# Attention scores in row pairs and values in float32: one edit of a diffusion block on one core

## The chip, the cores and the metric

The kernel runs on one core of one Trainium2 chip. The metric is the device time of one execution, in microseconds (us). A measurement is a set of runs; the median and the ends are given. Beside them stands one execution that the hardware profiler took; the rows in this document come from that one.

## What is computed

Two layers work on 512 latent tokens and 256 context tokens of width 1024. The edit lies in the first layer's token mixer, differential attention with 8 heads: each head has two maps of 64 dimensions, whose softmaxes are taken one from the other. Cut to what matters:

```python
def attend(qb, kk, vv):
    s = jnp.einsum('bqhmd,bkhmd->bhmqk', qb, kk).astype(jnp.float32) * scale
    p = jax.nn.softmax(s, axis=-1)
    p = p[:, :, 0] - lam_full * p[:, :, 1]
    return jnp.einsum('bhqk,bkhe->bqhe', p.astype(vv.dtype), vv)
```

Here m is the map (0 or 1), d runs over 64, k over 768 keys (512 latent, 256 context) and e over the 128 columns of a head's values. Only latent queries (512) matter. After it come an RMS norm of each head's output, the output projection, a SwiGLU FFN, and a second layer with a short convolution and another FFN.

## The kernel before, in words

Everything is float32. For speed the matmuls run on the one-pass type fp32r, and each operand is split in a high part (rounded to fp32r, on ScalarE, ACT) and a low part (the rest, on VectorE, DVE): `split`, L53 to L55. A product is then three matmuls, high x high, high x low and low x high: `mm3`, L77 to L80.

The stages in order of time: modulation weights, norms and transposes of the inputs with the projections of head 0 (to some 104 us of the profiled execution); the attention of 8 heads with the projections of later heads and the output projection between (to some 420 us); then FFN, convolution and FFN, which are long streams of matmuls.

One head of the attention (`attend`, L508) loops over two halves of the queries (`pr`), and in each over two blocks of 128 queries (`s`), so that there are 32 blocks in all. For a block and each of the two maps, four matmuls write the scores S (128 queries x 768 keys, in two ranges of columns, 512 and 256, in two PSUM banks); DVE takes the negative maximum of a row (L532); ACT takes the exponential and its sum (L536). DVE then adds the two maps with their weights (L546), six transposes on TensorE (PE) bring the result to keys x queries (L551), and `split` writes its two parts `pth` and `ptl` (L553). After two blocks the values are multiplied: 6 blocks of keys x `mm3` of 256 columns into `po` (L556 to L558), copied to O by ACT.

How S is computed before: a map has only 64 dimensions, so the 128 rows of a matmul hold two things. `finish_q` (L442) and `finish_k` (L451) apply the rotary positions (`rope`, with POOL, that is GpSimd, and DVE), split the result into `qt` and `kt`, and `halves_to` (L432) copies the parts by eight DMAs for a head on SyncE's queue (SP): `qs0` and `qs1` hold a map's q twice, one above the other, high parts and low parts side by side; `ks0` and `ks1` hold the high part of k in the upper 64 rows and the low part in the lower. One matmul of 128 rows so gives q_high x (k_high + k_low), a second q_low x (k_high + k_low).

The values of two heads at a time are projected by `proj_v_steps` and split by `finish_v` (L461) into `vh` and `vl`, six tiles each. Head 0 and the first values come from PSUM of the first stage.

PSUM has eight banks: two buffers of two banks for S, two for the accumulators of projections ("acc"), two for transposes, `po` and small things ("pt").

What sets the order: nothing is written out by hand. The generators in `todo` (projections of the next heads, modulation vectors `ada_steps`, the output projection `wo_steps`) are stepped through after each head in the program's text, and a scheduler in the framework, which works with modelled times, mixes all instructions into one fixed order for each engine ahead of the run. Each engine then works its list in that order. All loads and copies are issued from SP's queue, in order too.

Of the kernel before, what the change touches and what calls it, by code (L numbers as in the profile page):

```python
# [11 lines left out]
F32 = mybir.dt.float32  # L12
F32R = mybir.dt.float32r
# [5 lines left out]
P = 128  # L19
# [5 lines left out]
def block_kernel(  # L25
# [11 lines left out]
    nc = tc.nc  # L37
    T = x.shape[1]
# [4 lines left out]
    KV = T + C  # L43
    KB = KV // P
# [8 lines left out]
    def split(hi, lo, src):  # L53
        nc.scalar.copy(hi, src)  # L54
        nc.vector.tensor_tensor(lo, src, hi.bitcast(F32), op=ALU.subtract)  # L55
# [21 lines left out]
    def mm3(ps, sh, sl, mh, ml, start, stop):  # L77
        nc.tensor.matmul(ps, sh, mh, start=start, stop=False)  # L78
        nc.tensor.matmul(ps, sh, ml, start=False, stop=False)  # L79
        nc.tensor.matmul(ps, sl, mh, start=False, stop=stop)  # L80
# [30 lines left out]
    psB = tc.alloc_tile_pool(name="psB", bufs=2, space=PSUM)  # L111
# [8 lines left out]

    for tag, n, bufs in (
        [(f"Or{h}", 512, 1) for h in range(NH)] + [("qs0", 1024, 2), ("qs1", 1024, 2)]
        + [("e", 768, 3), ("pth", 768, 3), ("ptl", 768, 3), ("ks0", 768, 2), ("ks1", 768, 2)]
        + [(f"v{p}{t}", 256, 2) for t in range(KB) for p in "hl"]
        + [("sq", 512, 1), ("dg0", 512, 1), ("dg1", 512, 1)]
        + [(t, 4, 2) for t in ("sv", "sr", "rh", "rl")] + [(t, 4, 3) for t in ("rr", "mx")] + [("ss", 8, 2), ("den", 8, 2)]
        + [("ld", 2, 1)]
        + [("araw", 1024, 2), ("ada", 1024, 1), ("qt", 1024, 1), ("kt", 1536, 1), ("rcos", 512, 1), ("rsin", 512, 1)]
        + [("sw", 512, 1), ("rt", 512, 2)]
    ):  # L130
        ap.tile([P, n], F32, tag=tag, bufs=bufs, name=f"place_{tag}")
# [4 lines left out]
    xt_dram = nc.dram_tensor("xt_spill", [DB, P, T], F32, kind="Internal").ap()  # L136

    rows = lambda v: v.rearrange("(j p) -> j p", p=P)
    st1, st2 = (ap.tile([P, P], F32, tag=t, name=n) for t, n in (("ks1", "st1"), ("ks1", "st2")))
    nc.vector.memset(st1, 0.0)  # L140
    nc.vector.memset(st2, 0.0)
    nc.sync.dma_start(st1[0:8, :], rows(c[0]))
# [26 lines left out]
    cn = [nat(ctx, t, "qs1", 2, f"cn{t}") for t in range(CB)]  # L169
# [37 lines left out]
    def nat_rstd(src, tag, name):  # L207

        nb = len(src)
        ss = ap.tile([P, 8], F32, tag="ss", name=f"ss{name}")  # L210
        for t in range(nb):
            for f in range(2):
                junk = ap.tile([P, 512], F32, tag="sq", bufs=1, name=f"junk{name}")
                nc.scalar.activation(
                    junk, src[t][:, f * 512:(f + 1) * 512], AF.Square,
                    accum_out=ss[:, t + 4 * f:t + 4 * f + 1],
                )
        v = ap.tile([P, 4], F32, tag="sv", name=f"sv{name}")[:, :nb]
        nc.vector.tensor_tensor(v, ss[:, :nb], ss[:, 4:4 + nb], op=ALU.add)
        nc.vector.tensor_scalar(v, v, 1.0 / D, EPS, op0=ALU.mult, op1=ALU.add)  # L220
        r = ap.tile([P, 4], F32, tag="sr", name=f"sr{name}")[:, :nb]
        nc.gpsimd.tensor_tensor(r, v, mhalf[:, :nb], op=ALU.pow)
        ps = spread(r, nb, "pt", name)
        o = ap.tile([P, 512], F32, tag=tag, bufs=2 if tag == "ks0" else 1, name=f"rs{name}")[:, :nb * P]
        nc.vector.tensor_copy(o, ps)
        return o

# [40 lines left out]
    for k in range(0, DB, 2):  # L268
        pt = psB.tile([P, 2, T], F32, tag="S", name=f"ptx{k}")
# [3 lines left out]
            nc.vector.tensor_copy(XT0[k + a], pt[:, a, :])  # L273
        if k == 0:
            ada0(0, raws0)
    rc = nat_rstd(cn, "ks0", "c")
    ctt = [ap.tile([P, 4, C], F32, tag="araw", name=f"ct{i}") for i in range(2)]
    CT = [ctt[k // 4][:, k % 4, :] for k in range(DB)]
    for i in range(2):
        pt = psB.tile([P, 4, C], F32, tag="S", name=f"ptc{i}")  # L280
        for a in range(4):
            k = 4 * i + a
# [146 lines left out]
        eng.tensor_tensor(r, r, s, op=ALU.add)  # L429
        return r  # L430

    def halves_to(dst, src, both):  # L432

        for m in range(2):
            s = src[64 * m:64 * m + 64]
            for d in range(2):
                o = dst[m][64 * d:64 * d + 64]
                nc.sync.dma_start(
                    o.bitcast(F32), (s if both else s[:, d, :]).bitcast(F32)
                )  # L440

    def finish_q(h, ps):  # L442

        r = rope(ps, HD ** -0.5, f"q{h}")
        qt = ap.tile([P, 2, T], F32R, tag="qt", bufs=1, name=f"qt{h}")
        split(qt[:, 0, :], qt[:, 1, :], r)
        q = [ap.tile([P, 2, T], F32R, tag=f"qs{m}", name=f"qs{h}_{m}") for m in range(2)]
        halves_to(q, qt, True)
        return q

    def finish_k(h, ps, psc):  # L451

        r = rope(ps, None, f"k{h}")
        kt = ap.tile([P, 2, KV], F32R, tag="kt", bufs=1, name=f"kt{h}")
        split(kt[:, 0, T:], kt[:, 1, T:], psc)
        split(kt[:, 0, :T], kt[:, 1, :T], r)
        ks = [ap.tile([P, KV], F32R, tag=f"ks{m}", name=f"ks{h}_{m}") for m in range(2)]
        halves_to(ks, kt, False)
        return ks

    def finish_v(g, t, ps):  # L461
        vh = ap.tile([P, 256], F32R, tag=f"vh{t}", name=f"vh{g}_{t}")
        vl = ap.tile([P, 256], F32R, tag=f"vl{t}", name=f"vl{g}_{t}")
        split(vh, vl, ps)
        return vh, vl

    def v_load(g):
        cols = slice(2 * D + 256 * g, 2 * D + 256 * (g + 1))
# [39 lines left out]
    def attend(h, between, after=None):  # L508
        q, ks, vs = Q[h], K[h], V[h // 2]
        vc = slice((h % 2) * P, (h % 2) * P + P)  # L510
        O = ap.tile([P, T], F32, tag=f"Or{h}", bufs=1, name=f"O{h}")
        den = ap.tile([P, 2, TB], F32, tag="den", name=f"den{h}")
        for pr in range(2):
            pts = []
            for kh in range(2):
                pts.append(
                    (ap.tile([P, 3, 256], F32R, tag="pth", bufs=3, name=f"pth{h}_{pr}_{kh}"),
                     ap.tile([P, 3, 256], F32R, tag="ptl", bufs=3, name=f"ptl{h}_{pr}_{kh}"))
                )
            for s in range(2):  # L520
                qb = 2 * pr + s
                e = []
                mx = ap.tile([P, 2], F32, tag="mx", bufs=3, name=f"mx{h}_{qb}")
                for m in range(2):
                    S = psB.tile([P, 1024], F32, tag="S", name=f"S{h}_{qb}_{m}")
                    for a, b in ((0, 512), (512, KV)):
                        for j in range(2):
                            nc.tensor.matmul(  # L528
                                S[:, a:b], q[m][:, j, qb * P:(qb + 1) * P], ks[m][:, a:b],
                                start=(j == 0), stop=(j == 1),  # L530
                            )
                    nc.vector.tensor_reduce(  # L532
                        out=mx[:, m:m + 1], in_=S[:, :KV], axis=AX.X, op=ALU.max, negate=True
                    )
                    em = ap.tile([P, KV], F32, tag="e", bufs=3, name=f"e{h}_{qb}_{m}")
                    nc.scalar.activation(  # L536
                        em, S[:, :KV], AF.Exp, bias=mx[:, m:m + 1], accum_out=den[:, m, qb:qb + 1]
                    )
                    e.append(em)

                rr = ap.tile([P, 1], F32, tag="rr", bufs=3, name=f"rr{h}_{qb}")
                nc.vector.reciprocal(rr, den[:, 1, qb:qb + 1])
                nc.vector.scalar_tensor_tensor(
                    rr, rr, nlam, den[:, 0, qb:qb + 1], op0=ALU.mult, op1=ALU.mult
                )
                nc.vector.scalar_tensor_tensor(e[0], e[1], rr, e[0], op0=ALU.mult, op1=ALU.add)  # L546
                for kh in range(2):
                    pt = psB.tile([P, 512], F32, tag="pt", name=f"pt{h}_{qb}_{kh}")[:, :3 * P]
                    for i in range(3):
                        k = 3 * kh + i  # L550
                        nc.tensor.transpose(pt[:, i * P:(i + 1) * P], e[0][:, k * P:(k + 1) * P], ident)  # L551
                    cs = slice(s * P, (s + 1) * P)
                    split(pts[kh][0][:, :, cs], pts[kh][1][:, :, cs], pt.rearrange("p (k c) -> p k c", c=P))  # L553
                between()
            po = psB.tile([P, 512], F32, tag="pt", name=f"po{h}_{pr}")[:, :256]
            for k in range(KB):  # L556
                ph, pl = pts[k // 3]
                mm3(po, vs[k][0][:, vc], vs[k][1][:, vc], ph[:, k % 3, :], pl[:, k % 3, :], k == 0, k == KB - 1)  # L558
            nc.scalar.copy(O[:, pr * 256:(pr + 1) * 256], po)
            if after:  # L560
                On[h] = O
                after(pr, den)
        On[h] = O
        if not after:
            later.append(subnorm(h, den, 0, TB))
# [395 lines left out]
```

## Time and profile before

| what | value |
|---|---|
| median of 3 runs | 1371.27 us (1370.04 to 1371.96) |
| the profiled execution | 1369.84 us |
| its span, first to last instruction | 1368.1 us |
| mean granted clock of PE in it | 0.987 of full |
| PE, DVE, ACT, POOL busy | 96%, 57%, 39%, 18% of the span |

The profile's page has a table of engines with their busy time, and the span in 40 slices with a digit for each engine (9 is 90% or more). A timeline row has the start, the time until the end, the engine, the line, the operation with what it writes and reads, the tile of the array (rows*columns), the shape, and how many instructions were merged. PEld is the load of a matmul's stationary operand, which runs beside PE. Matmuls are pipelined: the next starts before the one ahead has ended, so the step from start to start is what a matmul costs.

### The profile page before, as it was taken

Reading aid. Unit: us, or ns where it says so; the run is one execution under the profiler, and the core shown is the slowest. Engines: PE = TensorE matmul, PEld = TensorE weight load, DVE = VectorE, ACT = ScalarE, POOL = GpSimd, SP = SyncE. Lnnn points to the kernel's source line nnn. Section 1 sums busy time; section 2 is a strip of 40 time slices with the busy share of each in tenths; the row PEclk is TensorE's granted clock in tenths of the full one; section 3 lists DMA queues with packets and bytes.
Section 4 is the critical chain, followed back from the end, with each engine's and each line's share of the span. In section 5 each row is a group of like instructions: output and inputs, shape, how many; then the busy total and the mean of one; then the engine's idle time right before and its main releaser. Section 6 shows DMA issues by size and latency. Waiting matters only on the chain.

```text
span 1368.1 us, 18008 instructions
## 1 busy us (share of the span) xinstructions
PE 1312.1 (96%) x7052; PEld 1128.1 (82%) x7052; DVE 780.4 (57%) x1043; ACT 529.6 (39%) x872; POOL 244.8 (18%) x197
## 2 busy tenths in 40 slices
PE   6889899899999999999999999999999999999997
PEld 4678799798888988888888889888988888888887
DVE  6886976777886766776753255444473333332322
ACT  6655646454555432333222244222362232232222
POOL 3244635524314100000001041000340000000000
PEclk9999999999999999999999999999999999999999
DMA  8957633623432666666643333333333333333321
GB/s 291 271 151 219 189 101 124 152 80 93 135 97 80 197 206 200 219 222 203 212 128 96 100 93 93 93 98 88 92 93 99 102 92 93 106 91 109 94 78 62
DMA packets 238742, 182.79 MB, mean 134 GB/s; under 512 B 6937, under 2 KB 220226, under 8 KB 238658
## 3 DMA queue, kind: packets, MB, share of 16 engines
q1 hardware_dynamic: 238658, 181.65, 44.7%
q8 instruction: 55, 0.90, 0.3%
q14 instruction: 29, 0.24, 0.1%
HBM read 162.75 MB, written 4.19 MB: 122 GB/s over the span
## 4 chain that ended last, share of the span: by engine, by line
PE 79%; DVE 8%; DMA 4%; ACT 4%; issue 2%; POOL 2%; SPq 0%; DVEq 0%; ACTq 0%; POOLq 0%
PE po_fo L78 6%; PE po_fo L79 6%; PE po_fo L80 6%; PE pb L79 5%; PE pb L78 5%; PE pb L80 5%; PE pa L78 5%; PE pa L79 5%; PE pa L80 5%; DMA araw<-in_ada_w_dram 3%; PE S L528 2%; PE psc L79 1%; PE psb L80 1%; PE psu L80 1%; PE psc L80 1%
## 5 line engine op out<-in xcount | busy, mean ns | idle before, releaser
L54 ACT CAST whi_f<-raw_f 128x1024 fp32r<-128x1024 f32 x87 | 91.4, 1051 | 234.6 <-issue 117.9
L55 DVE TENSOR_TENSOR wlo_f<-raw_f,whi_f 128x1024 fp32r<-128x1024 f32 x87 | 107.4, 1234 | 79.2 <-ACT whi_f L54 76.2
L55 DVE TENSOR_TENSOR wlo_fo<-raw_fo,whi_fo 128x1024 fp32r<-128x1024 f32 (+1 forms) x48 | 54.5, 1135 | 118.4 <-ACT whi_fo L54 116.8
L607 POOL TENSOR_TENSOR nacc<-nacc,nsq 128x256 f32<-128x256 f32 x30 | 30.7, 1023 | 494.1 <-ACT nsq L603 493.6
L78 PE MATMUL po_fo<-uh,whi_fo 128*128 128x512 f32 (+1 forms) x324 | 118.8, 367 | 0.1
L79 PE MATMUL po_fo<-ul,whi_fo 128*128 128x512 f32 (+1 forms) x324 | 118.7, 366 | 0.0
L80 PE MATMUL po_fo<-uh,wlo_fo 128*128 128x512 f32 (+1 forms) x324 | 118.6, 366 | 0.0
L54 ACT CAST whi_fo<-raw_fo 128x1024 fp32r<-128x1024 f32 (+1 forms) x48 | 47.1, 981 | 177.6 <-PE po_fo L79 146.9
L378 DVE SCALAR_TENSOR_TENSOR ada<-araw,sil,ada 128x1024 f32<-128x1024 f32 x49 | 62.9, 1284 | 39.0 <-DMA araw<-in_ada_w_dram 38.7
L803 DVE TENSOR_TENSOR uu<-sl,pb 128x512 f32<-128x512 f32 (+1 forms) x48 | 30.7, 640 | 81.5 <-PE pb L80 77.2
L536 ACT ACTIVATE e<-S,mx 128x768 f32<-128x768 f32 x64 | 57.8, 904 | 46.7 <-DVE mx L532 36.1
L80 PE MATMUL pb<-h2h,wlo_f 128*128 128x512 f32 (+1 forms) x192 | 71.8, 374 | 0.0
L78 PE MATMUL pa<-h3h,whi_f 128*128 128x512 f32 (+1 forms) x192 | 71.6, 374 | 0.0
L79 PE MATMUL pb<-h2l,whi_f 128*128 128x512 f32 (+1 forms) x192 | 71.5, 372 | 0.0
L78 PE MATMUL pb<-h2h,whi_f 128*128 128x512 f32 (+1 forms) x192 | 71.4, 372 | 0.0
L78 PE MATMUL pb<-h3h,whi_f 128*128 128x512 f32 (+1 forms) x192 | 71.4, 372 | 0.0
L79 PE MATMUL pb<-h3l,whi_f 128*128 128x512 f32 (+1 forms) x192 | 71.4, 372 | 0.0
L80 PE MATMUL pa<-h3h,wlo_f 128*128 128x512 f32 (+1 forms) x192 | 71.4, 372 | 0.0
L80 PE MATMUL pb<-h3h,wlo_f 128*128 128x512 f32 (+1 forms) x192 | 71.4, 372 | 0.0
L79 PE MATMUL pa<-h3l,whi_f 128*128 128x512 f32 (+1 forms) x192 | 71.2, 372 | 0.0
L78 PEld LDWEIGHTS po_fo<-uh,whi_fo 128*128 128x128 f32 x324 | 61.2, 189 | 10.1 <-DVE on L890 0.3
L79 PEld LDWEIGHTS po_fo<-ul,whi_fo 128*128 128x128 f32 x324 | 61.1, 189 | 9.9
(362 smaller groups left out, 3715.2 us busy)
## 6 DMA issues: line engine op xcount, KB each, us to landing
raw_f<-in_ffn_w_in_dram SPq DMA_DIRECT2D x88, 512.0 KB, 3.6
araw<-in_ada_w_dram SPq DMA_DIRECT2D x80, 512.0 KB, 4.4
raw_fo<-in_ffn_w_out_dram SPq DMA_DIRECT2D x32, 512.0 KB, 3.7
raw_a<-in_ada_w_dram SPq DMA_DIRECT2D x32, 256.0 KB, 4.6
qs<-qt SPq DMA_DIRECT2D x32, 256.0 KB, 4.9
raw_wv<-in_da_wqkv_dram SPq DMA_DIRECT2D x12, 512.0 KB, 5.0
ks<-kt SPq DMA_DIRECT2D x32, 192.0 KB, 4.8
raw_fo<-in_ffn_w_out_dram SPq DMA_DIRECT2D x16, 384.0 KB, 4.0
```

The source lines that it names most:

```text
L54: nc.scalar.copy(hi, src)
L55: nc.vector.tensor_tensor(lo, src, hi.bitcast(F32), op=ALU.subtract)
L78: nc.tensor.matmul(ps, sh, mh, start=start, stop=False)
L79: nc.tensor.matmul(ps, sh, ml, start=False, stop=False)
L80: nc.tensor.matmul(ps, sl, mh, start=False, stop=stop)
L378: nc.vector.scalar_tensor_tensor(acc, raw, s, acc, op0=ALU.mult, op1=ALU.add)
L528: nc.tensor.matmul(S[:, a:b], q[m][:, j, qb * P:(qb + 1) * P], ks[m][:, a:b], start=(j == 0), stop=(j == 1),)
L536: nc.scalar.activation(em, S[:, :KV], AF.Exp, bias=mx[:, m:m + 1], accum_out=den[:, m, qb:qb + 1])
L607: nc.gpsimd.tensor_tensor(acc, acc, sq, op=ALU.add)
L803: nc.vector.tensor_tensor(u, s, pb, op=ALU.mult)
```

## The change

Three things change in the attention. First, the scores: `halves_to` and its DMAs go. `finish_q` and `finish_k` split into one tile each, whose partitions 0 to 63 belong to map 0 and 64 to 127 to map 1. The scores take three products (high x high, high x low, low x high) on the 64 rows of a map, and the matmuls of the two maps alternate, each into its own S tile; the block's 12 matmuls are put under a manual order for PE. The maxima and exponentials follow after both maps. Second, `finish_v` keeps the values in float32, by one copy on ACT. Third, the transposed weights are copied unsplit to float32, and one float32 matmul takes the place of `mm3`. The tags `ks0` and `ks1` become `kk` of twice the size, `qs1` and `ptl` keep their places for what else uses them, and two small tiles of the first stage (`st1`, `st2`, and the context's norm) change their tags.

```diff
-    def halves_to(dst, src, both):
...
     def finish_q(h, ps):
         r = rope(ps, HD ** -0.5, f"q{h}")
-        qt = ap.tile([P, 2, T], F32R, tag="qt", bufs=1, name=f"qt{h}")
-        split(qt[:, 0, :], qt[:, 1, :], r)
-        q = [ap.tile([P, 2, T], F32R, tag=f"qs{m}", name=f"qs{h}_{m}") for m in range(2)]
-        halves_to(q, qt, True)
+        q = ap.tile([P, 2, T], F32R, tag="qs0", bufs=2, name=f"q{h}")
+        split(q[:, 0, :], q[:, 1, :], r)
         return q
     def finish_k(h, ps, psc):
         r = rope(ps, None, f"k{h}")
-        kt = ap.tile([P, 2, KV], F32R, tag="kt", bufs=1, name=f"kt{h}")
-        split(kt[:, 0, T:], kt[:, 1, T:], psc)
-        split(kt[:, 0, :T], kt[:, 1, :T], r)
-        ks = [ap.tile([P, KV], F32R, tag=f"ks{m}", name=f"ks{h}_{m}") for m in range(2)]
-        halves_to(ks, kt, False)
+        ks = ap.tile([P, 2, KV], F32R, tag="kk", bufs=2, name=f"ks{h}")
+        split(ks[:, 0, T:], ks[:, 1, T:], psc)
+        split(ks[:, 0, :T], ks[:, 1, :T], r)
         return ks
     def finish_v(g, t, ps):
-        vh = ap.tile([P, 256], F32R, tag=f"vh{t}", name=f"vh{g}_{t}")
-        vl = ap.tile([P, 256], F32R, tag=f"vl{t}", name=f"vl{g}_{t}")
-        split(vh, vl, ps)
-        return vh, vl
+        v = ap.tile([P, 256], F32, tag=f"vh{t}", name=f"v{g}_{t}")
+        nc.scalar.copy(v, ps)
+        return v
...
-                for m in range(2):
-                    S = psB.tile([P, 1024], F32, tag="S", name=f"S{h}_{qb}_{m}")
+                Ss = [psB.tile([P, 1024], F32, tag="S", name=f"S{h}_{qb}_{m}") for m in range(2)]
+                with tc.manual_schedule(engines={mybir.EngineType.PE}):
                     for a, b in ((0, 512), (512, KV)):
-                        for j in range(2):
-                            nc.tensor.matmul(
-                                S[:, a:b], q[m][:, j, qb * P:(qb + 1) * P], ks[m][:, a:b],
-                                start=(j == 0), stop=(j == 1),
-                            )
+                        for j, (jq, jk) in enumerate(((0, 0), (0, 1), (1, 0))):
+                            for m in range(2):
+                                r = slice(64 * m, 64 * m + 64)
+                                nc.tensor.matmul(
+                                    Ss[m][:, a:b], q[r, jq, qb * P:(qb + 1) * P], ks[r, jk, a:b],
+                                    start=(j == 0), stop=(j == 2),
+                                )
+                for m, S in enumerate(Ss):
                     nc.vector.tensor_reduce(
...
-                    split(pts[kh][0][:, :, cs], pts[kh][1][:, :, cs], pt.rearrange("p (k c) -> p k c", c=P))
+                    nc.scalar.copy(pts[kh][:, :, cs], pt.rearrange("p (k c) -> p k c", c=P))
                 between()
...
             for k in range(KB):
-                ph, pl = pts[k // 3]
-                mm3(po, vs[k][0][:, vc], vs[k][1][:, vc], ph[:, k % 3, :], pl[:, k % 3, :], k == 0, k == KB - 1)
+                nc.tensor.matmul(po, vs[k][:, vc], pts[k // 3][:, k % 3, :], start=(k == 0), stop=(k == KB - 1))
```

## Rows read from the trace of the kernel before

**Rows 1.** The page: engines with busy us, share and instructions; PE's slices.

```profile
PE 1312.1 (96%) x7052; PEld 1128.1 (82%) x7052; DVE 780.4 (57%) x1043; ACT 529.6 (39%) x872; POOL 244.8 (18%) x197
...
PE   6889899899999999999999999999999999999997
```

**Rows 2.** Busy time by windows: length, PE, PEld, DVE, ACT, POOL, granted clock, DMA.

```profile
104.00:436.00 332.00, 309.11 (x1987) 279.49 (x1986) 255.18 (x408) 175.50 (x339) 143.27 (x103) 0.97 0.46 128
436.00:1368.10 932.10, 920.35 (x4575) 783.26 (x4573) 445.72 (x503) 290.01 (x428) 63.52 (x67) 1.00 0.41 124
```

**Rows 3.** Timeline of PE in a dense place: start, us, engine, line, operation.

```profile
383.56 0.39 PE L79 MATMUL poa<-o,whi_woa 128*128 128x512 f32 x1
383.79 0.39 PE L80 MATMUL poa<-o,wlo_woa 128*128 128x512 f32 x1
384.01 0.85 PE L528 MATMUL S<-ks,qs 128*128 128x512 f32 x4
384.70 0.28 PE L78 MATMUL po<-pth,vh 128*128 128x256 f32 x1
...
385.06 0.28 PE L78 MATMUL po<-pth,vh 128*128 128x256 f32 x1
```

**Rows 4.** Timeline of PE at the float32 matmuls of L605.

```profile
440.46 0.59 PE L605 MATMUL pn<-nsq,ones_f 128*128 128x256 f32 x2
440.70 0.47 PE L78 MATMUL pa<-h2h,win 128*128 128x256 f32 x1
441.01 0.60 PE L605 MATMUL pn<-nsq,ones_f 128*128 128x256 f32 x2
```

**Rows 5.** Timeline of PE and PEld at 4-row transposes, and after a wait.

```profile
40.74 0.28 PE L80 MATMUL vps<-ch,w0l 128*128 128x256 f32 x1
...
40.95 0.20 PEld L256 LDWEIGHTS pmt<-ident,mr 4*128 4x128 f32 x2
40.95 0.28 PE L256 MATMUL pmt<-ident,mr 4*128 4x4 f32 x2
...
41.16 0.08 PEld L248 LDWEIGHTS pm<-whi_a,cst 128*4 128x4 f32 x1
...
99.66 0.39 PE L78 MATMUL pskc<-ch,whi_wk 128*128 128x256 f32 x1 [1.00 <-ACT rtq L425]
...
99.88 0.28 PE L79 MATMUL pskc<-cl,whi_wk 128*128 128x256 f32 x1
```

**Rows 6.** PE's waits from 104 to 436 us: total us, times, longest.

```profile
PE psv L78 <- DVE kt L55: 5.7, 1, 5.7
PE S L528 <- ACT e L536: 5.4, 3, 3.7
PE poa L78 <- ACT o L54: 2.9, 1, 2.9
PE S L528 <- DMA ks<-kt: 2.8, 1, 2.8
PE spro L204 <- POOL dg0o L200: 2.5, 2, 1.7
```

**Rows 7.** Instructions by tile: ns min/median/max, first and last start, forms.

```profile
L55 DVE TENSOR_TENSOR ptl<-pt,pth x64: 532/547/558, 124.4 to 416.3; 128x384 fp32r<-128x384 f32 x64
...
L55 DVE TENSOR_TENSOR vl<-psv,vh x18: 401/414/426, 113.4 to 336.6; 128x256 fp32r<-128x256 f32 x18
L55 DVE TENSOR_TENSOR vl<-vps,vh x6: 399/410/425, 85.9 to 92.8; 128x256 fp32r<-128x256 f32 x6
```

**Rows 8.** DMA issues on the page: count, KB each, us to landing.

```profile
qs<-qt SPq DMA_DIRECT2D x32, 256.0 KB, 4.9
```

**Rows 9.** Instructions that read S: ns min/median/max, first and last start.

```profile
L532 DVE TENSOR_REDUCE mx<-S x64: 936/947/960, 111.4 to 401.8; 128x1 f32<-128x768 f32 x64
L536 ACT ACTIVATE e<-S,mx x64: 879/903/924, 112.4 to 403.8; 128x768 f32<-128x768 f32 x64
```

**Rows 10.** Timeline of DVE while PE waits at 243.6 us.

```profile
243.69 3.07 DVE L546 SCALAR_TENSOR_TENSOR e<-e,rr,e 128x768 f32<-128x768 f32 x1
```

More of the change, by code (lines that the diff above doesn't have):

```diff
@@ L122, in block_kernel @@
         [(f"Or{h}", 512, 1) for h in range(NH)] + [("qs0", 1024, 2), ("qs1", 1024, 2)]
-        + [("e", 768, 3), ("pth", 768, 3), ("ptl", 768, 3), ("ks0", 768, 2), ("ks1", 768, 2)]
+        + [("e", 768, 3), ("pth", 768, 3), ("ptl", 768, 3), ("kk", 1536, 2)]
         + [(f"v{p}{t}", 256, 2) for t in range(KB) for p in "hl"]
@@ L138, in block_kernel @@
     rows = lambda v: v.rearrange("(j p) -> j p", p=P)
-    st1, st2 = (ap.tile([P, P], F32, tag=t, name=n) for t, n in (("ks1", "st1"), ("ks1", "st2")))
+    st1, st2 = (ap.tile([P, P], F32, tag=t, name=n) for t, n in (("kk", "st1"), ("kk", "st2")))
     nc.vector.memset(st1, 0.0)
@@ L223, in nat_rstd @@
         ps = spread(r, nb, "pt", name)
-        o = ap.tile([P, 512], F32, tag=tag, bufs=2 if tag == "ks0" else 1, name=f"rs{name}")[:, :nb * P]
+        o = ap.tile([P, 512], F32, tag=tag, bufs=1, name=f"rs{name}")[:, :nb * P]
         nc.vector.tensor_copy(o, ps)
@@ L275, in block_kernel @@
             ada0(0, raws0)
-    rc = nat_rstd(cn, "ks0", "c")
+    rc = nat_rstd(cn, "kt", "c")
     ctt = [ap.tile([P, 4, C], F32, tag="araw", name=f"ct{i}") for i in range(2)]
@@ L430, in rope @@
         return r
-    def halves_to(dst, src, both):
-        for m in range(2):
[L435 to L439, printed above, removed]
-                )
     def finish_q(h, ps):
         r = rope(ps, HD ** -0.5, f"q{h}")
-        qt = ap.tile([P, 2, T], F32R, tag="qt", bufs=1, name=f"qt{h}")
-        split(qt[:, 0, :], qt[:, 1, :], r)
-        q = [ap.tile([P, 2, T], F32R, tag=f"qs{m}", name=f"qs{h}_{m}") for m in range(2)]
-        halves_to(q, qt, True)
+        q = ap.tile([P, 2, T], F32R, tag="qs0", bufs=2, name=f"q{h}")
+        split(q[:, 0, :], q[:, 1, :], r)
         return q
@@ L515, in attend @@
             for kh in range(2):
[L516 to L519, printed above, removed]
+                pts.append(ap.tile([P, 3, 256], F32, tag="pth", bufs=3, name=f"pth{h}_{pr}_{kh}"))
             for s in range(2):
@@ L523, in attend @@
                 mx = ap.tile([P, 2], F32, tag="mx", bufs=3, name=f"mx{h}_{qb}")
-                for m in range(2):
-                    S = psB.tile([P, 1024], F32, tag="S", name=f"S{h}_{qb}_{m}")
+                Ss = [psB.tile([P, 1024], F32, tag="S", name=f"S{h}_{qb}_{m}") for m in range(2)]
+                with tc.manual_schedule(engines={mybir.EngineType.PE}):
                     for a, b in ((0, 512), (512, KV)):
-                        for j in range(2):
-                            nc.tensor.matmul(
-                                S[:, a:b], q[m][:, j, qb * P:(qb + 1) * P], ks[m][:, a:b],
-                                start=(j == 0), stop=(j == 1),
-                            )
+                        for j, (jq, jk) in enumerate(((0, 0), (0, 1), (1, 0))):
[6 more added lines that the diff above has]
+                for m, S in enumerate(Ss):
                     nc.vector.tensor_reduce(
```

## The prediction

> **What bounds the kernel now.** I read the page first: the table of engines, then the slices. TensorE (PE) is busy for 96% of the span, VectorE (DVE) for 57%, and PE's digits stay at 8 and 9 from the second slice on [rows 1]. So the kernel is bound by PE, unless PE stands still somewhere. Next I cut the span into three stretches with the view of busy time by windows. From 436 us on, PE misses 11.8 of 932 us and the granted clock is 1.00: nothing of the change lies there, and nothing is to be had. The change lies in 104 to 436 us, the attention. There PE misses 22.9 of 332 us, and the mean granted clock is 0.97, which is about 10 us of full rate lost (0.03 x 332), since of the two levels 1.2 GHz does half the work. DVE is busy for 255 of the 332 us [rows 2]. So the stage has a PE bound of some 300 us and some 33 us in which PE waits or runs slowly. An edit can act on either.
>
> Third, PE's timeline in a dense place gives the prices. The steps from start to start are what counts, not the durations, which overlap. A matmul of 512 columns takes 0.23 us, one of 256 takes 0.12; the four matmuls of a map's scores take 0.69 (2 x 0.23 + 2 x 0.12); three matmuls of the values take 0.36 [rows 3]. Last, the waits of PE in the stage: a DMA of the keys (2.8 us), DVE's split of the keys (5.7), the exponential on ScalarE (ACT) (5.4), ACT's split of O (2.9) and a diagonal of GpSimd (POOL) (2.5) [rows 6].
>
> **The scores, as matmuls.** A block is one row block of queries: two maps, two ranges of columns. Before it issues 8 matmuls on all 128 rows, 4 x (0.23 + 0.12) = 1.40 us. After it issues 12 on 64 rows, in 6 pairs. There are 32 blocks. No row of before shows two matmuls side by side, so I bound it from both sides. If a pair costs one slot, a block takes 3 x 0.35 = 1.05 us, and 32 blocks save 11.2 us. If each matmul keeps a slot of its own, a block takes 2.10 and 32 blocks cost 22.4 us more. I take the first: the two of a pair share no row of the array, no partition of q or of the keys and no PSUM bank, and together they read what one 128-row matmul of [rows 3] reads in one slot. Their weight loads are a second unknown. A load that nothing hides costs 0.10 us: the first matmul after a wait starts 0.22 us before its successor, where 0.12 is usual [rows 5]. If a pair's two loads follow one another they need 0.21, which fits under 0.23 but not under 0.12, and the 96 pairs of 256 columns cost 0.09 more each, 8.9 us in all. I take nothing for it, as loads are hidden in every dense row, and keep 8.9 as an end.
>
> **The scores, as a change of the array's division.** The trace has one place where matmuls on few rows stand between full ones, the transposes of 4 rows at L256. There the next weight load does not start with the running matmul, as it usually does: the matmul of 40.74 ends at 41.02, and the load of the transposes comes at 40.95, 0.07 us before the end; the way back is the same, end 41.23, load 41.16 [rows 5]. A switch so costs the step from start to load, 0.21, less the usual 0.12, and the bare load of 0.10 to 0.11: about 0.20 us. Twice a block, 64 times, that is 12.8 us; the other end is nothing, if 64 rows are no change for the array, or if the block has to wait anyway. I take 12.8, by the row. The Trainium skill, "TensorEngine Tiling (Array Packing)", Key Properties, says that changing the tiling mode drains the engine, while different tiles of one mode load and multiply in parallel. By that rule the price of [rows 5] holds for 64 rows too; the rows agree for 4 rows, and no run here shows 64. The same sentence speaks for the first end of the pairs, which no row of before can show.
>
> **The weights times the values.** Three fp32r matmuls of 256 columns (0.36 us) become one in float32. The trace has such a one in L605, recorded as two instructions: with one fp32r matmul of 256 columns it takes 0.55 us (440.46 to 441.01) [rows 4], so 0.43 alone. There are 8 heads x 2 x 6 = 96, and 96 x 0.07 = 6.7 us more on PE. The trace has the very shape, so the ends are near, 6 to 8.
>
> **What DVE loses.** The low parts of the transposed weights go, 64 x 0.547 = 35.0 us, and those of V, 18 x 0.414 + 6 x 0.410 = 9.9 us [rows 7]. ACT's casts become copies of the same size and cost the same. 42.5 of these 44.9 us lie in the stage, a sixth of DVE's 255. DVE is not the bound, so this comes back only where PE waits for it.
>
> **The copies of q and k.** 64 DMAs go, 32 of q and 32 of k; one of q lands 4.9 us after its issue [rows 8]. The wait of 2.8 us ahead of the first scores ends with one of k [rows 6]. Without the copy the scores wait for the split itself, which is done a landing (4.9 us) earlier, so the whole 2.8 us go; next late there is nothing but PE's own order. The other copies are hidden behind the head before. All loads are issued on the same queue of SyncE (SP), so loads behind a copy no longer wait for its split; I count nothing for that.
>
> **The maxima.** Both maps' maxima now follow the whole block instead of starting when map 0 is done, and a block needs both S buffers free, not one. A maximum takes 0.947 us and an exponential 0.903; the 64 maxima are spread over 290 us, so a block comes each 9.2 us [rows 9]. From the end of a block to free buffers it is 2 x 0.95 + 0.90 + 0.2, some 3 us, and PE has projections for the rest. Nothing, as long as that cover is there; in the last head, which has no projections, it could be 3 us in each of 4 blocks, 12 us.
>
> **The waits that DVE makes.** Beside the DMA, four waits are in reach: 5.7 for the keys' split, 3.7 of the 5.4 for the exponential, 2.9 for O, 1.7 for the diagonal, 14 us [rows 6], and the 10 us of clock that PE loses after such pauses. In the longest DVE was late: during it a weighted sum of 128x768 took 3.07 us [rows 10], where a maximum over as many elements takes 0.95 [rows 9]. With a sixth of the work gone I take half of the 24, 12 us. The ends are none and all; and since the program's order is drawn up anew, new waits can take their place.
>
> **The sum** against the profiled execution (1369.84 us, its span 1368.1): -11.2 + 12.8 + 6.7 - 2.8 - 12.0 = -6.5, so 1363.3. That execution lies 1.43 below the median of 1371.27, so the median after is 1364.8. What a measurement of this kernel can tell from no change is 0.2%, 2.7 us.
>
> **The rivals.**
> Switching costs nothing: the sum without 12.8 is -19.3, 1352.0. For it: the row has 4 rows of the array, not 64, and 0.07 us of overlap already. Against it: the step is the same on both ways. Chance 0.20.
> The loads of a pair follow one another: +8.9, so +2.4, 1373.7. For it: a bare load costs 0.10 [rows 5], and one path for it would do for all rows before. Chance 0.16.
> The waits stay, or others come (the last head's wait for both S buffers first): +12, so +5.5, 1376.8. Chance 0.15.
> The pairs do not run side by side, and the change does not do what it says. That is slower: the scores cost 22.4 more instead of 11.2 less, +27.1, 1398.4. Its place is the 32 blocks, its price 0.70 us over before in each; it decides from the point where a fifth of the overlap is missing (6.5 of 33.6). Against it: nothing is shared; for it: no row shows two at once. Chance 0.15.
>
> **How the numbers follow.** The forecast has the rest, 0.34; its own range is 1357 to 1373. The range of 8 in 10 takes in the forecast, the free switches at 1352 with some more of the waits gone, and both small losses: 1347 to 1387. Left out is the case without overlap. Faster by over 0.2%: some 0.24 of the forecast, 0.19 of the second, 0.03 of the small losses: 0.46. Within 0.2%: 0.14. Slower: 0.40.
>
> **What would show it.** In the changed kernel's PE timeline a pair's two matmuls should start within 0.03 us of one another, and a block's 12 should take about 1.05 us; 1.35 would be loads in a row, 2.1 no overlap. The load ahead of a block and the one behind it should start 0.07 us before the previous matmul's end. The values should step at 0.43. DVE's busy time should fall by some 45 us, PE's misses in the stage from 23 us to about 12, and the granted clock there should rise above 0.97. If the misses grow, the sum is wrong in its largest guess.

## The result and the profile after

The changed kernel takes 1389.26 us (median of 4 runs, 1383.74 to 1390.87) against 1371.36 (4 runs, 1370.04 to 1371.96): a ratio of 1.0122, with a 95% interval of 1.0104 to 1.0139. It is slower by 18 us, where a gain of 6.5 was forecast, and it lies 2.3 us above the range. Its profiled execution took 1390.30 us (span 1388.5).

The page of the changed kernel, engines with busy time, share and instructions, beside [rows 1]:

```profile
PE 1342.2 (97%) x7084; PEld 1125.6 (81%) x7084; DVE 754.0 (54%) x955; ACT 529.9 (38%) x872; POOL 241.4 (17%) x197
```

PE is now busy for 30 us more, although a block's 6 pairs were to take 6 slots where 8 full matmuls took 8. DVE fell by 26.4 us. Next the same cut of the span as in [rows 2]: length, PE, PEld, DVE, ACT, POOL, granted clock, DMA.

```profile
104.00:436.00 332.00, 322.32 (x1896) 261.98 (x1893) 216.72 (x302) 167.03 (x317) 130.41 (x89) 0.97 0.27 82
436.00:456.00 20.00, 18.69 (x145) 17.85 (x144) 13.24 (x25) 10.51 (x25) 11.36 (x16) 1.00 0.19 65
456.00:1388.50 932.50, 920.35 (x4573) 782.39 (x4571) 445.75 (x502) 289.74 (x427) 63.30 (x67) 1.00 0.41 124
```

The last line has the same 920.35 us of PE as the stretch from 436 us on had before, so the feed-forward part is untouched and all of the loss lies ahead of it. In the attention PE now misses only 9.7 of 332 us, where it missed 22.9, and has still not finished its work. So PE does not wait more. It needs more time for what it does. PE's waits in the stage, beside [rows 6] (total us, times, longest):

```profile
PE S L513 <- ACT e L522: 3.6, 2, 2.3
PE psv L78 <- DVE ks L55: 2.9, 1, 2.9
PE pt L537 <- DVE sv L566: 1.0, 1, 1.0
PE spro L204 <- POOL dg0o L200: 0.7, 1, 0.7
```

The wait for the DMA of the keys is gone, and the others are about halved, much as forecast.

To put numbers to this I cut the profiled execution in the same way for every kernel: from 100 us to the start of the last matmul of the values, the idle time of PE added up from its records, half of the time that it ran at 1.2 GHz, and the rest, called **work** here. Before: 418.5 - 100 = 318.5 us, of which 22.0 idle and 20.5 at 1.2 GHz, so 32.2 **lost** and 286.3 of work. After: 436.7 - 100 = 336.7 us, 10.9 idle and 17.1 at 1.2 GHz, so 19.4 lost and 317.3 of work (each rounded by itself). Lost time fell by 12.8, and work grew by 31.0, which makes the +18.2 (the rest of the +20.5 between the two executions, 2.2 us, comes after that matmul). The forecast for work was -11.2 + 12.8 + 6.7 = +8.3. Some 23 us of work were not foreseen.

The PE timeline shows what they are. A block of scores in the changed kernel, start, length, line, operation:

```profile
141.72 0.39 PE L79 MATMUL psq<-hl,whi_wq 128*128 128x512 f32 x1
142.03 0.50 PE L513 MATMUL S<-ks,q 64*128 64x512 f32 x1
142.46 0.50 PE L80 MATMUL psq<-hh,wlo_wq 128*128 128x512 f32 x1
142.80 0.39 PE L78 MATMUL psq<-hh,whi_wq 128*128 128x512 f32 x1
143.02 0.39 PE L79 MATMUL psq<-hl,whi_wq 128*128 128x512 f32 x1
143.25 0.39 PE L80 MATMUL psq<-hh,wlo_wq 128*128 128x512 f32 x1
143.48 0.39 PE L78 MATMUL psk<-hh,whi_wk 128*128 128x512 f32 x1
143.79 1.07 PE L513 MATMUL S<-ks,q 64*128 64x512 f32 x7
144.80 0.88 PE L537 MATMUL pt<-ident,e 128*128 128x128 f32 x6
145.60 0.50 PE L513 MATMUL S<-ks,q 64*128 64x256 f32 x4
146.04 0.50 PE L79 MATMUL psk<-hl,whi_wk 128*128 128x512 f32 x1
```

The 12 matmuls of this block stand in three stretches, of 1, 7 and 4, with projections and transposes between them. The first one is alone: from 141.72 to 142.80 there are 1.08 us for two projection steps of 0.23 and one matmul of scores, so 0.62 for a matmul whose slot is 0.23. The 0.39 over are two changes of the array's division, 0.20 each, the price of [rows 5]. And the slot itself was to be shared with the partner, which comes 1.8 us later.

In all, the 384 matmuls stand in **82 stretches** instead of 32: none is a whole block of 12, 31 have a single matmul, and 60 have an odd number, so that one matmul of each has no partner beside it (**lone** below). The manual order keeps the 12 matmuls in order among themselves. It doesn't keep other PE work out of their midst. Nor was the partner held up on the chip. The two exponentials that free the S buffers for this block start here (start, length):

```profile
135.14 0.91 ACT L522 ACTIVATE e<-S,mx 128x768 f32<-128x768 f32 x1
136.39 0.92 ACT L522 ACTIVATE e<-S,mx 128x768 f32<-128x768 f32 x1
```

Both buffers were free from 137.3 on, 4.7 us before 142.03, and so they were at the first matmul of 27 of the 31 blocks that follow another. The partner came late because the order, fixed ahead of the run, had other work before it.

The values step as forecast. Six records, that is three float32 matmuls of two instructions each, and the full one behind them:

```profile
127.34 1.46 PE L544 MATMUL po<-pth,v 128*128 128x256 f32 x6
128.45 0.47 PE L78 MATMUL psv<-whi_wv,hh 128*128 128x256 f32 x1
```

In the single records the steps from the first to the sixth are 0.215 to 0.220 us, so 0.43 for the two instructions of one float32 matmul. The full matmul's record starts 0.03 after the sixth and is longer than usual by what is missing there (0.47 instead of 0.28).

### The profile page after: what moved, and what is told of

It is laid out like the page before. It is cut to its first block, busy times and chain, and to the rows that moved or that the text cites. A ratio compares the mean times of both kernels' runs of the same rounds, so it can differ in the third digit from the quotient of the medians.

```text
span 1388.5 us, 17807 instructions
## 1 busy us (share of the span) xinstructions
PE 1342.2 (97%) x7084; PEld 1125.6 (81%) x7084; DVE 754.0 (54%) x955; ACT 529.9 (38%) x872; POOL 241.4 (17%) x197
## 4 chain that ended last, share of the span: by engine, by line
PE 82%; DVE 7%; DMA 5%; ACT 2%; issue 1%; POOL 1%; SPq 1%; DVEq 0%; POOLq 0%; ACTq 0%
PE po_fo L78 6%; PE po_fo L80 6%; PE po_fo L79 6%; PE pb L79 5%; PE pb L78 5%; PE pb L80 5%; PE pa L78 5%; PE pa L79 5%; PE pa L80 5%; PE S L513 3%; DMA araw<-in_ada_w_dram 3%; PE po L544 3%; PE pt L537 1%; PE psv L78 1%; PE psv L79 1%
## 5 line engine op out<-in xcount | busy, mean ns | idle before, releaser
L518 DVE TENSOR_REDUCE mx<-S 128x1 f32<-128x768 f32 x64 | 58.1, 949 | 48.0 <-PE S L513 48.0
```

Of the source, the lines that this page charges most:

```text
L518: nc.vector.tensor_reduce(out=mx[:, m:m + 1], in_=S[:, :KV], axis=AX.X, op=ALU.max, negate=True)
```

## The experiments

**My theory after the result:** the prices were right and the count of passages was wrong; the broken blocks make the loss. **Rivals:** the 64-row matmuls are dear even in whole blocks; the float32 values make the loss; the waits that went were not DVE's.

**1. The scores alone.** The changed kernel with the split values and weights of before:

```diff
     def finish_v(g, t, ps):
...
-        nc.scalar.copy(v, ps)
-        return v
+        split(vh, vl, ps)
+        return vh, vl
...
-                nc.tensor.matmul(po, vs[k][:, vc], pts[k // 3][:, k % 3, :], start=(k == 0), stop=(k == KB - 1))
+                mm3(po, vs[k][0][:, vc], vs[k][1][:, vc], ph[:, k % 3, :], pl[:, k % 3, :], k == 0, k == KB - 1)
```

> The scores of the changed kernel, with values and weights split as before the change. Theory (the scheduler breaks the blocks of scores up; every passage between 64 and 128 rows costs TensorE about 0.2 us and a matmul whose partner is not beside it keeps a slot of its own): the scores alone carry the loss, 74 stretches of scores instead of 82, so about 14 x (74 - 64 + ...) nothing better: scores 28 us dearer than before, values 6.7 us cheaper than in the changed kernel, VectorE's 45 us back and with them part of the waits: 1385 to 1397 us. Rival (the float32 values are what costs, through TensorE or through ScalarE): close to the kernel before, 1366 to 1376 us.

Measured: 1384.51 us, ratio 1.0104 (1.0089 to 1.0119). That is 0.5 us under the lower end, with 74 stretches and 20.8 us more work than before. The scores carry the loss; the values as its cause fall.

**2. The values alone.** The kernel before with the other half:

```diff
...
-                    split(pts[kh][0][:, :, cs], pts[kh][1][:, :, cs], pt.rearrange("p (k c) -> p k c", c=P))
+                    nc.scalar.copy(pts[kh][:, :, cs], pt.rearrange("p (k c) -> p k c", c=P))
...
-                mm3(po, vs[k][0][:, vc], vs[k][1][:, vc], ph[:, k % 3, :], pl[:, k % 3, :], k == 0, k == KB - 1)
+                nc.tensor.matmul(po, vs[k][:, vc], pts[k // 3][:, k % 3, :], start=(k == 0), stop=(k == KB - 1))
```

> The kernel before with float32 values and weights alone. Theory: TensorE gets 96 x 0.07 = 6.7 us more, VectorE 45 us less; if half of the waits and of the slow clock go as in the changed kernel (idle fell there from 23 to 10 us), 1371 + 6.7 - 10 = 1368 us, between 1362 and 1374. Rival (the float32 values carry the loss): 1380 us or more.

Measured: 1365.87, ratio 0.9968 (0.9942 to 0.9993), with +4.4 of work and lost time down from 32.2 to 24.6. This half by itself is a gain: PE pays some 4 us and gets more than that back from waits.

**3. Whole blocks.** The changed kernel, where a block's first matmul waits for the exponential that frees the second S buffer, and its 12 go ahead of other PE work:

```diff
-                with tc.manual_schedule(engines={mybir.EngineType.PE}):
+                with tc.high_priority(), tc.manual_schedule(engines={mybir.EngineType.PE}):
...
-                                nc.tensor.matmul(
+                                mm = nc.tensor.matmul(
...
+                                if prev_exp and a == j == m == 0:
+                                    tc.add_manual_dep(
+                                        mm.ins, prev_exp[-1].ins.name,
...
+                                    )
```

> The changed kernel, with the first matmul of a block made to wait for both S buffers and the block's matmuls given the highest priority, so that the program has 35 stretches of scores (29 of all 12 matmuls) instead of 82. Theory: 47 stretches less x 0.4 us = 19 us, and some 49 matmuls find their partner, x 0.175 us = 8.6 us; together 27 us, 1389 - 27 = 1362 us (1356 to 1370). Rival (the blocks wait for both buffers, and this wait or something else carries the loss): 1385 us or more, with TensorE idle ahead of the scores.

Measured: 1363.43, ratio 0.9951 (0.9934 to 0.9969). Now there are 35 stretches, 29 of them whole blocks, and no matmul is lone. Its PE timeline:

```profile
197.57 0.28 PE L78 MATMUL psv<-whi_wv,hh 128*128 128x256 f32 x1
197.78 1.31 PE L514 MATMUL S<-ks,q 64*128 64x512 f32 x12
199.02 0.55 PE L545 MATMUL pt<-ident,e 128*128 128x128 f32 x3
```

and its first pair, from a shorter window of the same view:

```profile
197.78 0.50 PE L514 MATMUL S<-ks,q 64*128 64x512 f32 x2
```

Two matmuls of 512 columns lie within 0.50 us, where the first one after a change takes 0.50 alone (142.03 above): they run at the same time. In the records that the view adds up, the starts of a pair lie 0 to 4 ns apart, those of their two weight loads 0 to 3 ns, and pairs follow each other at 0.23 us for 512 columns and 0.115 for 256. The block starts at 197.78, 0.07 before the matmul ahead of it ends (197.57 + 0.28). The twelve take 1.24 us to the next engine work, which is 3 x (0.23 + 0.115) = 1.04, a bare load of 0.10 and the way out. Against the values alone this kernel has 292.3 - 290.6 = 1.7 us more of work; the forecast for pairs and passages together was -11.2 + 12.8 = +1.6. So the sum of the scores' prices fits whole blocks, to within the 3.6 us by which work also moved between two orders of the same matmuls (experiment 7).

**4. One map after the other.** Experiment 3 with another order of the same 12 matmuls:

```diff
-                    for a, b in ((0, 512), (512, KV)):
-                        for j, (jq, jk) in enumerate(((0, 0), (0, 1), (1, 0))):
-                            for m in range(2):
+                    for m in range(2):
+                        for a, b in ((0, 512), (512, KV)):
+                            for j, (jq, jk) in enumerate(((0, 0), (0, 1), (1, 0))):
```

> As the kernel with the blocks together, but the six matmuls of map 0 come first and then the six of map 1, so no two neighbours lie on different rows except at the middle. Theory (two matmuls on different rows share a slot): a block takes some 2.1 instead of 1.05 us, 32 x 1.0 = 32 us more than with the maps alternating, about 1394 us. Rival (pairs gain nothing): the same time as with the maps alternating.

Measured: 1382.87 (one execution), 19.0 above the profiled execution of experiment 3, 19.6 in work. The pairs do give time, but I had expected more. The timeline shows why:

```profile
201.32 0.28 PE L78 MATMUL psv<-whi_wv,hh 128*128 128x256 f32 x1
201.53 1.90 PE L514 MATMUL S<-ks,q 64*128 64x512 f32 x12
203.37 0.55 PE L545 MATMUL pt<-ident,e 128*128 128x128 f32 x3
```

A block takes 1.84 us, not 1.24 + 1.04 = 2.28. In the records map 1's first matmul starts 6 ns after map 0's third, while map 0's three of 256 columns are still ahead in the program: the two halves of the array's rows then work side by side again. 32 x (1.84 - 1.24) = 19.2 is about the whole difference.

**5. Whole blocks, split values.** Experiment 3 with the values and weights of before:

```diff
-        nc.scalar.copy(v, ps)
-        return v
+        split(vh, vl, ps)
+        return vh, vl
...
-                nc.tensor.matmul(po, vs[k][:, vc], pts[k // 3][:, k % 3, :], start=(k == 0), stop=(k == KB - 1))
+                mm3(po, vs[k][0][:, vc], vs[k][1][:, vc], ph[:, k % 3, :], pl[:, k % 3, :], k == 0, k == KB - 1)
```

> Blocks together (33 stretches of scores in the program), values and weights split as before the change. Theory (what float32 costs TensorE, 6.7 us, VectorE's freed 45 us give back in waits): 1363 - 6.7 + 12 = 1368 us, 1361 to 1374. Rival (VectorE's work does not matter here): 1357 us.

Measured: 1365.98, ratio 0.9965 (0.9949 to 0.9981). Work is +0.4 on the kernel before: the 64-row scores, passages included, cost PE nothing more when the blocks hold together.

**6. VectorE freed, PE unchanged.** The kernel before without the low parts of the values and of the transposed weights: the three matmuls all read high parts, so the result lacks the low parts.

```diff
-        split(vh, vl, ps)
-        return vh, vl
+        nc.scalar.copy(vh, ps)
+        return vh, vh
...
-                    split(pts[kh][0][:, :, cs], pts[kh][1][:, :, cs], pt.rearrange("p (k c) -> p k c", c=P))
+                    nc.scalar.copy(pts[kh][0][:, :, cs], pt.rearrange("p (k c) -> p k c", c=P))
```

> The kernel before without the low parts of the weights and the values: VectorE's 45 us of subtractions go, TensorE keeps three matmuls, all of high parts, in their place. The low parts are left out of the result. Theory (freeing VectorE takes half of TensorE's waits and of the slow clock away): 1370 - 12 = 1358 us, 1352 to 1364. Rival (VectorE's work does not matter): 1370 us.

Measured: 1369.04, ratio 0.9996 (0.9978 to 1.0014). A miss: DVE loses the same subtractions, and the time stays. Lost time is 32.3 us, against 32.2 before. PE's waits in its stage, the two longest:

```profile
PE psv L78 <- ACT rtk L423: 6.1, 1, 6.1
PE pt L547 <- DVE O L581: 3.4, 1, 3.4
```

The waits of [rows 6] for the keys' split and O's split became shorter or went, and a wait of 6.1 us for ACT's copy of the keys ahead of their rotation stands where there was none of that size. The order was drawn up anew and is late at another place.

**7. The subtractions kept.** Experiment 2 with the two subtractions still made, into tiles that nothing reads:

```diff
         nc.scalar.copy(v, ps)
+        nc.vector.tensor_tensor(vl, ps, v, op=ALU.subtract)
...
+                    nc.vector.tensor_tensor(ptl[kh][:, :, cs], pt.rearrange("p (k c) -> p k c", c=P), pts[kh][:, :, cs], op=ALU.subtract)
```

> The kernel before with float32 values and weights, and VectorE's subtractions kept, though nothing reads them. Theory: TensorE's 6.7 us without the waits that VectorE's relief takes away: 1370 + 6.7 = 1377 us, 1371 to 1382. Rival (VectorE's work does not matter): 1366 us, as with the float32 values alone.

Measured: 1372.94, ratio 1.0024 (1.0012 to 1.0036), 7 us above experiment 2. With PE's float32 matmuls in place, the work taken from DVE came with these 7 us; in experiment 6 it came with none. The runs give it no price of its own apart from the order that it meets. Of the 7 us, 2.9 are lost time and 3.6 are work, though PE's matmuls are the same as in experiment 2: why was not tested, and it shows how far work alone moves with the order.

**8. More passages.** Experiment 3 with one full matmul of two columns between a block's two ranges, into columns of S that nothing reads:

```diff
+                        if a:
+                            nc.tensor.matmul(Ss[0][:, 1000:1002], ones_r, ones_r[:, 0:2], start=True, stop=True)
```

> The changed kernel with its blocks together, and one 128-row matmul of 2 columns between a block's two ranges, which doubles the passages between 64 and 128 rows (the program has 70 stretches of scores). Theory: 2 x 0.20 us for the passages and some 0.11 for the matmul, 32 x 0.5 = 16 us more than with the blocks together, 1380 us. Rival (a passage costs nothing; the broken pairs made the loss): 32 x 0.11 = 3.5 us more, 1367 us.

Measured: 1377.52, ratio 1.0048 (1.0024 to 1.0072), 14.1 us above experiment 3 (13.5, when each is taken from the kernel before that was measured with it), with 70 stretches. Its timeline:

```profile
203.22 0.28 PE L80 MATMUL psv<-whi_wv,hl 128*128 128x256 f32 x1
203.43 0.96 PE L516 MATMUL S<-ks,q 64*128 64x512 f32 x6
204.32 0.27 PE L512 MATMUL S<-ones_r 128*128 128x2 f32 x1
204.52 0.62 PE L516 MATMUL S<-ks,q 64*128 64x256 f32 x6
205.07 0.55 PE L547 MATMUL pt<-ident,e 128*128 128x128 f32 x3
```

The block takes 205.07 - 203.43 = 1.64 us instead of 1.24, 0.40 more, and 13.5 to 14.1 over the 35 further stretches are 0.39 to 0.40 each. These 0.40 are the way out and in again, with all pairs whole, together with whatever the matmul of two columns takes itself, which no run separates. This is the most direct measure of the price.

**9 and 10. The two edits of experiment 3, each alone:** the wait without the priority (9), and the priority without the wait (10). Against the changed kernel:

```diff
+                                if prev_exp and a == j == m == 0:
+                                    tc.add_manual_dep(
+                                        mm.ins, prev_exp[-1].ins.name,
...
+                                    )
```

> The changed kernel with the wait for both S buffers alone, without the priority: the program has 50 stretches of scores and 20 matmuls without a partner. Theory (a stretch costs 0.4 us, a matmul alone half a slot too much): against the blocks together (35 stretches, none alone) 15 x 0.4 + 10 x 0.2 = 8 us more, 1371 us. Rival (the priority is what helps, by way of the maxima's earlier start): no better than the changed kernel, 1385 us or more.

```diff
-                with tc.manual_schedule(engines={mybir.EngineType.PE}):
+                with tc.high_priority(), tc.manual_schedule(engines={mybir.EngineType.PE}):
```

> The changed kernel with the priority alone, without the wait for both S buffers: 66 stretches, 56 matmuls without a partner, since map 0's first matmul goes as soon as its own buffer is free. Theory: 31 x 0.4 + 28 x 0.23 = 19 us more than with the blocks together, 1382 us. Rival (the wait for both buffers is a cost and no help): 1363 us or less.

Measured: for the wait alone 1372.33, ratio 1.0016 (1.0002 to 1.0029), with 50 stretches and 20 lone matmuls; for the priority alone 1384.06, ratio 1.0101 (1.0077 to 1.0125), with 66 and 56. The priority alone leaves nearly all the lone ones. The wait takes away two thirds of them. The likely reason is that without it map 0's first matmul is put down where, in the modelled times of the order, its own S buffer is free, and map 1's only where the second one is, with projections between; the modelled times are on no record, and on the chip both buffers were free at 142.03. Only both together keep nearly all blocks whole.

**11. The copies put back.** Experiment 3 with the 64 DMAs of q and k issued again, into tiles that nothing reads:

```diff
         split(q[:, 0, :], q[:, 1, :], r)
+        halves_to([ap.tile([P, 2, T], F32R, tag="qs1", bufs=2, name=f"qd{h}_{m}") for m in range(2)], q, True)
         return q
...
         split(ks[:, 0, :T], ks[:, 1, :T], r)
+        kd = ap.tile([P, 2, KV], F32R, tag="kt", bufs=1, name=f"kd{h}")
+        halves_to([kd[:, m, :] for m in range(2)], ks, False)
         return ks
```

> Blocks together (38 stretches), and the 64 DMAs of q and k put back with the sizes of before, into tiles that nothing reads. Theory (the copies hold up the loads behind them on SyncE's queue, and so waits of TensorE): 1363 + 1 + 3 = 1367 us, up to 1373. Rival (only the wait ahead of the first scores was ever theirs): 1364 to 1365 us.

Measured: 1374.71, ratio 1.0041 (1.0023 to 1.0058), 11.3 us above experiment 3 (10.4, each from its own kernel before) and above what I had allowed. Work is +2.0, lost time +8.4, though no matmul reads a copy. Two waits of SP's queue, and two of PE, in this kernel:

```profile
SPq L439 <- DVE q L55: 51.6, 8, 8.7
SPq L439 <- ACT ks L54: 17.7, 6, 7.2
```

```profile
PE psq L78 <- ACT v L463: 3.6, 1, 3.6
PE psv L78 <- ACT rtk L424: 2.7, 1, 2.7
```

L439 is the copies' issue here. SP's queue stands for 69 us on copies whose source is not ready, with the loads of weights behind them; and the DMA share of 104 to 420 us is 0.48 against 0.30 in experiment 3. Yet all waits of the queue from 95 to 420 us add up to 253 us here and to 291 in experiment 3, where it stands longer on loads, so the 69 us are not simply time added. Queue, DMA share and the new order could each delay loads; the runs do not separate these.

**12. Full-row scores put first.** Experiment 2 with a map's four 128-row matmuls put ahead of other work, to see if the priority is a gain by itself:

```diff
-                    for a, b in ((0, 512), (512, KV)):
...
+                    with tc.high_priority():
+                        for a, b in ((0, 512), (512, KV)):
```

> The kernel before with float32 values, and its 128-row scores given the highest priority (58 stretches in place of 69; no passage between 64 and 128 rows in it). Theory (stretches cost nothing where all matmuls have 128 rows, so only waits can change): 1366 us as without the priority, within 4 us. Rival (an unbroken block is worth something by itself, through the earlier maxima): 1360 us or less.

Measured: 1372.28, ratio 1.0013 (0.9996 to 1.0030): slower than experiment 2 by 6.4 us (5.6, each from its own kernel before), outside the 4 us that I had allowed. Work is nearly the same (291.2 against 290.6). Lost time is 33.5 against 24.6, in a profiled execution that itself lies 6.7 above the median. So the priority is no gain by itself with 128-row scores; what experiment 3 wins fits the wholeness of its blocks, as the table shows.

**All of them side by side**, from the profiled executions (us). The last two columns stand against whole blocks with the same values: experiment 3, or experiment 5 for the scores alone. The count is 0.4 us for each stretch more and 0.086 for each lone matmul, half of a mean slot, (0.23 + 0.115) / 4. It is an estimate from the steps and passages above.

| kernel | lost | work | stretches / lone | work over whole blocks | by count |
|---|---|---|---|---|---|
| before | 32.2 | 286.3 | - | | |
| after | 19.4 | 317.3 | 82 / 60 | 25.0 | 24.0 |
| 3 whole blocks | 18.7 | 292.3 | 35 / 0 | 0 | 0 |
| 8 more passages | 19.6 | 307.6 | 70 / 0 | 15.2 | 14.0 |
| 9 wait alone | 18.5 | 302.1 | 50 / 20 | 9.7 | 7.7 |
| 10 priority alone | 19.5 | 311.4 | 66 / 56 | 19.1 | 17.2 |
| 11 copies back | 27.1 | 294.3 | 38 / 0 | 2.0 | 1.2 |
| 1 scores alone | 24.4 | 307.1 | 74 / 56 | 20.4 | 21.2 |
| 5 whole, split values | 31.1 | 286.7 | 33 / 0 | 0 | 0 |
| 2 values alone | 24.6 | 290.6 | - | | |
| 7 subtractions kept | 27.5 | 294.2 | - | | |
| 6 VectorE freed | 32.3 | 284.8 | - | | |
| 12 scores first | 33.5 | 291.2 | - | | |

Six kernels follow the count within 2 us. A dash stands for scores on 128 rows, which have no passages. Experiment 3 beats both kernels, by 0.5% and 1.7% (1 - 0.9951 / 1.0122).

## Why the prediction was wrong

**The step that failed** is "Twice a block, 64 times, that is 12.8 us", and with it that a pair always costs one slot. The price of a passage was right; the blocks' wholeness was taken from the diff's manual order. The trace counts 82 stretches, so 164 passages instead of 64, and 60 lone matmuls. By the count that is 24.0 us over whole blocks; measured are 25.0. In experiment 3, where the step nearly holds (70 passages, no lone matmul), the time is 6.4 us below the kernel before that was measured with it, where 6.5 were forecast. That it fits so closely is in part luck: work came to +6.0 instead of +8.3, and the -13.5 of lost time instead of -14.8 is not shown to have the reasons that the forecast gave (below).

**The pairs, -11.2: right.** The two matmuls and their loads go side by side. Each number that the prediction named holds in whole blocks: within 0.03 us of one another, about 1.05 us for the twelve without the passages, the load 0.07 before the end of the matmul ahead.

**The passage, 0.20: right**, by 0.39 for the two around a lone matmul and by 0.40 for the two of experiment 8. It was read from 4-row transposes, and their way back leads in [rows 5] to matmuls on four columns (128*4, L248), not to full ones as the prediction has it. So that it held for 64 rows between full ones was not given by the row. The Trainium skill, "TensorEngine Tiling (Array Packing)", Key Properties, says that a change of mode drains the engine, and that tiles of one mode load and multiply in parallel: the trace agrees with both at 64 rows, by the load 0.07 us before the previous matmul's modelled end and by pairs in one slot.

**The values, +6.7: right within 2.4 us.** +4.4 in experiment 2, 292.3 - 286.7 = 5.6 between experiments 3 and 5, +7.9 in experiment 7. The step, 0.43, is as forecast.

**DVE's work, 45 us less: too much.** The page shows 26.4 less. The subtractions of the weights and of V are gone. But the page counts time with two DVE records at once only once; the lengths of all records, added up, fell by 34.8 (826.0 to 791.2), so some 8 of the 45 us lay beside other records. The other 10 are DVE instructions that got longer, above all those on `rr`, by 4.3: before, first line, and after, second line (busy us and mean ns behind the bar):

```profile
L543 DVE SCALAR_TENSOR_TENSOR rr<-rr,nlam,den 128x1 f32<-128x1 f32 x32 | 14.2, 444 | 0.8
```

```profile
L529 DVE SCALAR_TENSOR_TENSOR rr<-rr,nlam,den 128x1 f32<-128x1 f32 x32 | 18.5, 578 | 1.1
```

The same 32 instructions took 444 ns and now take 578. In experiment 3 they take 453, so it is not the change as such that makes them longer. Why was not tested.

**The waits, -14.8 with the DMA: near in size, the reason not shown.** Lost time fell by 12.8. But DVE's relief alone gave 0 (experiment 6) or 7.6 (experiment 2, 32.2 to 24.6), the copies' removal alone 1.1 (experiment 5) or 7.8 (experiment 1), and the two together 13.5 (experiment 3). "I count nothing" for SP's queue is in doubt too: with the copies back, 8.4 us are lost that no reader of a copy explains, but not shown to be the queue's. How much belongs to which stays open, since each edit also draws up a new order, and an order alone moved lost time by 9 us in the one execution of experiment 12. The clock in the stage was to rise above 0.97; the view still rounds it to 0.97 (20.5 us at 1.2 GHz before, 17.1 after).

**The maxima after the whole block: right to cost nothing to PE, as far as its waits show.** PE waits 3.6 us for exponentials, less than the 5.4 of [rows 6]. DVE waits 48.0 us for S in 104 to 456 us, which costs only where PE then waits for DVE.

**The rivals.** Loads one after the other: no, they start together. Switching for nothing: no. No overlap: false as a mechanism, as experiment 3's pairs show, though the loss arose at its place, the 32 blocks; its price of 0.70 us a block over before came out nearly, as 20.8 / 32 = 0.65 in experiment 1, for another reason. The case that happened, a block broken up by other work of the same engine, was not among the rivals, although the prediction called on exactly that work as the cover of the maxima ("PE has projections for the rest"). That other matmuls were ready at that very moment was the warning.

## What to carry to other kernels

When a matmul's form has a price on entry and exit, count the stretches in the order that will be run, not the blocks in the source. An order that binds some instructions among themselves says nothing of what may come between, and where such a block needs two buffers, tie its first instruction to both and put it ahead of other work: here only the two together kept the blocks whole. Freeing an engine that isn't the bound may give nothing or several us, as the new order has it: of such a gain the range should hold all, including none.

## What was not expected of the hardware

- **A half of the rows goes ahead by itself.** With map 0's six matmuls queued ahead of map 1's six, map 1's first started 6 ns after map 0's third (experiment 4), and a block took 1.84 us instead of 2.28. So 0.44 of the 1.04 us that pairs save come without any alternating order.
- **Two weight loads at once.** Loads for the two halves start 0 to 3 ns apart (experiment 3), while the only bare load of before took 0.10 us [rows 5].
- **A matmul of two columns for 0.40 us.** Between 64-row matmuls, a full one that computes almost nothing costs nearly as much as two of 512 columns, 0.46 (experiment 8).
- **Copies that nobody reads came with 8 us** of lost time (experiment 11); what of it is the copies' and what the new order's stays open.
